# Ten of the 22 gate and value pairs of an up projection computed in seven block products

## The chip, the cores and the metric

One Trainium2 chip, one of its cores. The metric is device time in microseconds, from the start to the end of one execution; shorter is better. The engines are named as in the profile: PE is TensorE (matmuls), PEld its weight loads, DVE VectorE, ACT ScalarE, POOL GpSimd, SP SyncE, which only issues DMAs here.

## What is computed

One layer of an encoder: 512 tokens, 1024 columns, float32. Three sub-layers follow each other, each with a norm before and after and a residual x: token mixing (attention and a gated scan side by side), cross-attention into 256 memory tokens, and a gated MLP with a convolution over positions. The change is in the last one:

```
def conv_ffn(h, w_up, conv_w, conv_b, w_down):
    u = h @ w_up                                    # 512x1024 @ 1024x5632
    up = jnp.pad(u, ((0, 0), (1, 1), (0, 0)))
    acc = conv_b
    for j in range(3):
        acc = acc + up[:, j:j + n] * conv_w[j]
    gate, val = jnp.split(acc, 2, axis=-1)          # 2816 columns each
    return (jax.nn.silu(gate) * val) @ w_down
```

## The kernel before

**Three matmuls for one product.** Every float32 operand is split into a high part (a cast on ScalarE, L111) and a low part (what is left, on VectorE, L112); `mm3` (L185) then does high x high, high x low and low x high.

**Weights come in units.** The host packs nearly all weights into units of 128 x 1024 floats (512 KB). `unit` (L179) takes the next one and lets `issue_ahead` (L175) split units up to three ahead. `issue` (L154) loads a unit on SyncE's queue into a raw tile (`rawp`, two buffers, L140 to L151) and splits it into wh and wl (`wp`, four buffers). 110 units hold the weights up to the up projection, and 42 the products of the down projection. Units 50 to 57 are the queries of cross-attention, 58 to 65 its output projection, 66 to 109 the up projection.

**The up projection.** A tile of the result has 128 columns as partitions and the 512 tokens along its row. There are 22 pairs of a gate tile and a value tile; a tile is 8 blocks of the model dimension x 3 matmuls of 512 columns into one PSUM bank. The first two pairs are computed in two halves of 256 tokens, since the last two blocks of h are transposed (`turn_in`, L224) between their first halves. Then a plain loop over i = 2 to 21 does gate and value of a pair. `conv` (L983) takes each bank: bias and middle tap on ScalarE (L986), the other taps on VectorE (L987, L989), then silu on the gate (L992) or the product with the gate (L1000).

**The down projection** is already computed in seven block products (Strassen-Winograd): `PRODUCTS` names the weight block or sum of blocks of each. The sums of its weight blocks, t1 to t4, are made in DRAM by `new_sums` (L935) after pairs 2, 5, 8 and so on: the first block is copied by ScalarE's queue (t1, t3) or the sum before is copied by GpSimd's (t2, t4), and the second block is added by an accumulating DMA of GpSimd. `group_sides` (L948) makes the sums of the activations for eight pairs at a time.

**What sets the order.** The framework turns the text into one instruction list per engine and adds all waits; among ready instructions the one that is earlier in the text goes first, so instructions of one engine can change places. `tc.issue_after` pins an instruction behind another one on its engine. Of the 8 KB tiles `big` there are 16; of PSUM banks eight, two for each of the tags b, s, c, o. The residual x lies in two `big` tiles from the mixing on to the end.

## Time and profile before

| | |
|---|---|
| median of 3 runs | 828.1 us (827.95 to 830.31) |
| the profiled execution | 828.14 us, of which span 826.4 us |
| instructions | 11158 |
| DMA | 135.64 MB in 40054 packets, mean 164 GB/s |
| HBM | read 130.72 MB, written 25.17 MB |
| weight loads by SyncE (raw<-in_w) | 109 of 512 KB, median 3.9 us from issue to landing |
| first block copied by ScalarE's queue (sum_t<-in_wd) | 10 of 512 KB, 5.1 us |
| accumulating DMAs of GpSimd (sum_t<-in_wd) | 20 of 512 KB, 8.1 us |
| copies of a sum by GpSimd (sum_t<-sum_t) | 10 of 512 KB, 4.6 us |

How to read it: a row of a group of instructions has its line, engine, operation, out<-in with shapes and the count, then busy us and the mean ns of one, then the engine's idle time before it and who ended that. A row of a window has for each engine the busy us and the count, then the granted clock of TensorE (1.00 is full), the mean busy share of the 16 DMA engines, and GB/s. A row of the timeline has start, duration, engine and line. "DMA to landing" has minimum, median and maximum of the time from issue to the last byte. Matmuls are pipelined, and the records of two that follow each other overlap.

### The profile page before, as it was taken

The page shows a single profiled execution, that of the slowest core. Times are in us where ns is not written, and L with a number is a line of the kernel's source. Part 1 is how long each engine was busy: PE and PEld are TensorE (multiplying, and loading weights), DVE is VectorE, ACT ScalarE, POOL GpSimd, SP SyncE. Part 2 cuts the span into 40 slices and gives each one's busy share as a digit, 9 for nine tenths or more (in the row PEclk, how much of TensorE's full clock was granted, in tenths as well). Part 3 has the DMA queues.
Part 4 walks back from the last instruction along what each step waited for, and adds up shares of the span by engine and source line. Part 5 has one row for each costly group of instructions (what it writes and reads, how often), then busy time and mean ns, then how long its engine had stood idle before and what let it go on. Part 6 is the DMA issues. An engine that isn't in the chain of part 4 may idle for free.

```text
span 826.4 us, 11158 instructions
## 1 busy us (share of the span) xinstructions
PE 812.9 (98%) x4238; PEld 689.2 (83%) x4238; DVE 533.9 (65%) x802; ACT 456.3 (55%) x766; POOL 131.4 (16%) x194
## 2 busy tenths in 40 slices
PE   9999999999999999999999999999999999999996
PEld 7878888889898887888888898888888888888884
DVE  5347486569886875855453866557555655888765
ACT  6576756369788874645543554334333343567651
POOL 0110211044223201300000300111111121011302
PEclk9999999999999999999999999999999999999999
DMA  8696754667768533252213136797888996268852
GB/s 317 184 276 136 166 116 98 129 141 158 161 153 182 124 126 130 77 178 77 77 52 102 44 110 179 214 246 201 229 211 228 257 257 167 90 203 270 246 148 102
DMA packets 40054, 135.64 MB, mean 164 GB/s; under 512 B 5120, under 2 KB 7168, under 8 KB 39808
## 3 DMA queue, kind: packets, MB, share of 16 engines
q1 hardware_dynamic: 25632, 86.03, 30.5%
q0 software_dynamic: 11344, 40.38, 26.2%
q10 hardware_dynamic: 3024, 8.53, 3.0%
q8 instruction: 33, 0.54, 0.3%
q14 instruction: 21, 0.17, 0.1%
HBM read 130.72 MB, written 25.17 MB: 189 GB/s over the span
## 4 chain that ended last, share of the span: by engine, by line
PE 91%; DVE 3%; issue 2%; DMA 1%; ACT 1%; POOL 1%; POOLq 0%; DVEq 0%; ACTq 0%
PE ps_b L187 9%; PE ps_b L188 9%; PE ps_b L186 9%; PE ps_s L187 6%; PE ps_s L188 6%; PE ps_s L186 6%; PE ps_o L186 5%; PE ps_o L187 5%; PE ps_o L188 5%; PE ps_c L187 5%; PE ps_c L186 5%; PE ps_c L188 5%; PE ps_c L553 3%; PE ps_o L798 2%; PE ps_s L776 2%
## 5 line engine op out<-in xcount | busy, mean ns | idle before, releaser
L112 DVE TENSOR_TENSOR wl<-raw,wh 128x1024 fp32r<-128x1024 f32 (+1 forms) x93 | 112.2, 1208 | 117.5 <-ACT wh L111 117.3
L111 ACT CAST wh<-raw 128x1024 fp32r<-128x1024 f32 (+1 forms) x93 | 96.0, 1033 | 138.4 <-PE ps_b L187 44.0
L186 PE MATMUL ps_b<-big,wh 128*128 128x512 f32 (+1 forms) x320 | 118.2, 369 | 0.8 <-DVE big L112 0.8
L188 PE MATMUL ps_b<-big,wl 128*128 128x512 f32 (+1 forms) x320 | 116.6, 365 | 0.0
L187 PE MATMUL ps_b<-big,wh 128*128 128x512 f32 (+1 forms) x320 | 116.4, 364 | 0.0
L186 PEld LDWEIGHTS ps_b<-big,wh 128*128 128x128 f32 x320 | 60.4, 189 | 9.7 <-DVE big L112 0.9
L188 PEld LDWEIGHTS ps_b<-big,wl 128*128 128x128 f32 x320 | 60.3, 188 | 9.3
L187 PEld LDWEIGHTS ps_b<-big,wh 128*128 128x128 f32 x320 | 60.4, 189 | 9.1
L579 DVE TENSOR_TENSOR big<-big 128x512 f32<-128x512 f32 x64 | 48.4, 761 | 16.3 <-PE ps_c L553 9.4
L186 PE MATMUL ps_s<-wh,big 128*128 128x512 f32 (+1 forms) x140 | 53.7, 384 | 0.4 <-DVE big L112 0.4
L187 PE MATMUL ps_s<-wl,big 128*128 128x512 f32 (+1 forms) x140 | 53.2, 380 | 0.9 <-DMA wl<-in_w_dram 0.9
L188 PE MATMUL ps_s<-wh,big 128*128 128x512 f32 (+1 forms) x140 | 53.1, 379 | 0.0
L163 ACT CAST wh<-raw 128x1024 fp32r<-128x1024 f32 x35 | 36.8, 1050 | 25.9 <-PE ps_b L187 13.1
L168 POOL DMA_DIRECT2D wl<-in_w_dram x35 | 30.7, 877 | 121.3 <-ACT wl L165 106.3
L112 DVE TENSOR_TENSOR big<-ps_o,big 128x512 fp32r<-128x512 f32 x54 | 37.1, 688 | 13.4 <-ACT big L111 13.2
L111 ACT CAST big<-ps_o 128x512 fp32r<-128x512 f32 x54 | 31.7, 586 | 19.5 <-PE ps_o L901 7.5
L945 POOL DMA_DIRECT2D sum_t<-in_wd_dram x24 | 19.6, 831 | 125.1 <-DMA sum_t<-in_wd_dram 76.1
L186 PE MATMUL ps_o<-wh,big 128*128 128x512 f32 (+1 forms) x102 | 39.4, 386 | 0.0
L992 ACT ACTIVATE tmp<-tmp 128x512 f32<-128x512 f32 x22 | 13.9, 632 | 44.7 <-DVE tmp L989 44.7
L187 PE MATMUL ps_o<-wl,big 128*128 128x512 f32 (+1 forms) x102 | 38.2, 375 | 0.0
L188 PE MATMUL ps_o<-wh,big 128*128 128x512 f32 (+1 forms) x102 | 38.2, 374 | 0.0
L186 PE MATMUL ps_b<-wh,big 128*128 128x512 f32 x92 | 36.9, 402 | 0.0
(267 smaller groups left out, 2062.6 us busy)
## 6 DMA issues: line engine op xcount, KB each, us to landing
raw<-in_w_dram SPq DMA_DIRECT2D x109, 512.0 KB, 3.9
wl<-in_w_dram POOLq DMA_DIRECT2D x35, 512.0 KB, 5.6
sum_t<-in_wd_dram POOLq DMA_DIRECT2D x20, 512.0 KB, 8.1
sum_t<-in_wd_dram ACTq DMA_DIRECT2D x10, 512.0 KB, 5.1
sum_t<-sum_t POOLq DMA_DIRECT2D x10, 512.0 KB, 4.6
big<-sum_t SPq DMA_DIRECT2D x10, 512.0 KB, 4.4
raw<-sum_t SPq DMA_DIRECT2D x10, 512.0 KB, 4.5
big<-in_x_dram SPq DMA_DIRECT2D x8, 512.0 KB, 6.4
```

The costliest lines, as they stand in the source:

```text
L111: nc.scalar.copy(hi, src)
L112: (eng or nc.vector).tensor_sub(lo, src, hi.bitcast(F32))
L163: nc.scalar.copy(wh, raw)
L168: nc.gpsimd.dma_start(wl, io["w"][i], accum_op=ALU.add)
L186: nc.tensor.matmul(o, a[0], b[0], start=start, stop=False)
L187: nc.tensor.matmul(o, a[0], b[1], start=False, stop=False)
L188: last_mm[0] = nc.tensor.matmul(o, a[1], b[0], start=False, stop=stop).ins
L553: nc.tensor.matmul(o[:, b, :], kc[:, blk(b)], pat(qk, b * P, [[2 * m, P // (2 * m)], [T + m, 2], [1, m]]), start=True, stop=True)
L579: nc.vector.tensor_tensor(out=c, in0=c, in1=pat(tt, toff + off, [[2, npair], [gap, 2], [0, m]]), op=ALU.mult)
L776: nc.tensor.matmul(s, qT[h // 4][:, h % 4, blk(qb)], kT[:, 2 * (h // 4) + c, :], start=c == 0, stop=c == 1)
L798: nc.tensor.matmul(o, vv[:, c, h // 4].rearrange("p a d -> p (a d)"), pt[:, j, c, :], start=c + j == 0, stop=c == 3 and j == 1)
L945: nc.gpsimd.dma_start(t, weight_block(second_name, width(u)), accum_op=ALU.add)
```

## The change

Ten pairs (`UP_S`) are computed in seven products as well. The tokens are halved (near, far) and so is the model dimension; gate and value are the two column halves. w11 and w12 are the gate and value blocks of the first half of the model dimension, w21 and w22 those of the second; t1 = w11 + w12, t3 = w22 + w12, t2 = w22 + t1, t4 = w21 + t2. On the side of h there are four sums s1 to s4, made once on VectorE from `fulls`, an unsplit copy of the transposed h that ScalarE now keeps in `turn_in`, and split. Each product is 4 x 3 matmuls of 256 columns. Three banks hold a pair: g (w11, later w21 on top of it, and t4), m (t1, t2), n (w22, t3). VectorE and ScalarE put the products together, and `conv` runs as before, the gate from the bank, the value from a tile.

What the change moves besides:

- The units of these pairs hold two blocks of 256 KB each (the fourth one block). Loads run up to five units ahead, with the two `tmp4` tiles as two more raw buffers.
- The sums of weight blocks, of both projections, become a list of jobs: seeds (a copy of the first block, on SyncE's queue, pinned behind the last weight load) and adds (GpSimd, accumulating), for two pairs or two units of the down projection at a time, eight seeds and then eight adds. Five jobs go with each of units 53 to 60, three with each from unit 70 on. Rows of the sums in DRAM are 32 floats longer than their data.
- x is copied to DRAM by ScalarE's queue after the first two pairs and read back at product 4 of the down projection.
- The first left side of the down projection is made at i = 20, not at i = 8; banks go round by `next_bank`; the host packs the blocks of the ten pairs as `wu`.

```diff
@@ -26,12 +26,18 @@
...
-N_WHOLE, N_UNITS = 110, 152
+UP_S = (4, 6, 7, 9, 11, 12, 14, 16, 17, 19)
+N_MIX, N_WHOLE = 66, 110 - 2 * len(UP_S)
+N_DOWN = N_WHOLE + 4 * len(UP_S)
+N_UNITS = N_DOWN + 42
...
-SUMS = (("t1", "w11", "w12"), ("t3", "w22", "w12"), ("t2", "t1", "w22"), ("t4", "t2", "w21"))
-LAY_AHEAD = 3
+SUMS = (("t1", "w11", "w12"), ("t3", "w22", "w12"), ("t2", "w22", "t1"), ("t4", "w21", "t2"))
+BLOCKS = ("w11", "w12", "w21", "w22")
+UP_PRODUCTS = ("w11", "t2", "t1", "w22", "t3", "w21", "t4")
+JOBS_AHEAD, JOBS_UP, FIRST_JOB, LAST_JOB = 5, 3, 53, 60
+LAY_AHEAD, LOAD_AHEAD = 3, 5
@@ -116,45 +122,76 @@
...
+    def up_block(name, q):
+        if name in BLOCKS:
+            return io["wu"][q, BLOCKS.index(name)]
+        return sums[name, q]
...
+    plan = [[("w", i)] for i in range(N_MIX)]
+    whole = N_MIX
+    for i in range(NF):
+        if i in UP_S:
+            q = UP_S.index(i)
+            for k in range(0, 7, 2):
+                plan.append([("u", q, name) for name in UP_PRODUCTS[k:k + 2]])
+        else:
+            plan += [[("w", whole)], [("w", whole + 1)]]
+            whole += 2
...
+        k = (i - N_DOWN) % 4
+        if k >= 2 and N_MIX + 6 <= i < N_DOWN:
+            return tmp4([P, 1024])
...
     def load_w():
-        i = issued[0]
+        i = loaded[0]
...
-        issued[0] += 1
+            last_load[0] = nc.sync.dma_start(raw, weight_block(PRODUCTS[p][0], cols)).ins
+        elif plan[i][0][0] == "w":
+            last_load[0] = nc.sync.dma_start(raw, io["w"][plan[i][0][1]]).ins
+        else:
+            for k, (_, q, name) in enumerate(plan[i]):
+                while (name, q) not in sums and name not in BLOCKS:
+                    jobs.popleft()()
+                last_load[0] = nc.sync.dma_start(raw[:, half(k)], up_block(name, q)).ins
+            raw = raw[:, :512 * len(plan[i])]
+        loaded[0] += 1
         return raw
...
     def issue():
         i = issued[0]
-        raw = load_w()
+        issued[0] += 1
+        raw = raws.popleft() if raws else load_w()
@@ -169,12 +206,58 @@
...
+        n = JOBS_AHEAD if FIRST_JOB <= i <= LAST_JOB else JOBS_UP if i >= N_MIX + 4 else 0
+        for _ in range(min(n, len(jobs))):
+            jobs.popleft()()
+
+    def sum_jobs(name, n, block):
+        made = {}
+
+        def seed(out_name, first_name):
+            def go():
+                t = dram.tile([P, n + 32], F32, name="sum_%s_%s" % (out_name, name), tag="sum_%s_%s" % (out_name, name))
+                made[out_name] = t[:, :n]
+                with tc.issue_after(last_load[0]):
+                    nc.sync.dma_start(made[out_name], block(first_name))
+            return go
+
+        def add(out_name, second_name, keep):
+            def go():
+                src = made[second_name] if second_name in made else block(second_name)
+                nc.gpsimd.dma_start(made[out_name], src, accum_op=ALU.add)
+                keep(out_name, made[out_name])
+            return go
+        return seed, add
+
+    def plan_sums(rows):
+        made = [sum_jobs(name, n, block) + (keep,) for name, n, block, keep in rows]
+        for out_name, first_name, _ in SUMS:
+            for seed, _, _ in made:
+                jobs.append(seed(out_name, first_name))
+        for out_name, _, second_name in SUMS:
+            for _, add, keep in made:
+                jobs.append(add(out_name, second_name, keep))
...
+    for q in range(0, len(UP_S), 2):
+        plan_up_sums(range(q, min(q + 2, len(UP_S))))
+    for u in range(0, 6, 2):
+        plan_down_sums((u, u + 1))
...
             issue()
+        while N_MIX + 4 <= taken[0] and loaded[0] < min(N_UNITS, taken[0] + LOAD_AHEAD):
+            raws.append(load_w())
@@ -182,10 +265,15 @@
...
+    def mm3(o, a, b, start, stop, again=False):
+        nc.tensor.matmul(o, a[0], b[0], start=start, stop=False, skip_group_check=again)
+        nc.tensor.matmul(o, a[0], b[1], start=False, stop=False, skip_group_check=again)
+        last_mm[0] = nc.tensor.matmul(o, a[1], b[0], start=False, stop=stop, skip_group_check=again).ins
@@ -221,14 +306,14 @@
...
-    def turn_in(h, act, b, tags, before=None):
+    def turn_in(h, act, b, tags, keep=None):
         for c in range(2):
-            if before:
-                before(c)
             o = bank(tags[c]).rearrange("p (k n) -> p k n", k=4)
             for k in range(4):
                 nc.tensor.transpose(o[:, k, :], h[:, blk(c * 4 + k)], ident)
             hi, lo = act.hi, act.lo
+            if keep:
+                nc.scalar.copy(keep[c][:, :, blk(b)], o)
             if len(hi) == 2:
@@ -928,22 +1013,11 @@
...
     hT = new_act()
-    turns = res_second(ox, range(4), kv["x0"], between(x, g_post, g_pre, hT))
+    fulls = [big([P, 4, T]) for _ in range(2)]
+    turns = res_second(ox, range(4), kv["x0"], between(x, g_post, g_pre, hT, fulls))
...
-
-    def new_sums(u):
-        n = width(u).stop - width(u).start
-        for out_name, first_name, second_name in SUMS:
-            t = dram.tile([P, n], F32, name="sum_%s_%d" % (out_name, u), tag="sum_%s_%d" % (out_name, u))
-            if first_name in sums:
-                nc.gpsimd.dma_start(t, weight_block(first_name, width(u)))
-            else:
-                with tc.issue_after(last_act[0]):
-                    nc.scalar.dma_start(t, weight_block(first_name, width(u)))
-            nc.gpsimd.dma_start(t, weight_block(second_name, width(u)), accum_op=ALU.add)
-            sums.setdefault(out_name, []).append(t)
...
-            if i == 8:
+            if i == 20:
                 lay_ahead(1)
@@ -1016,11 +1090,74 @@
...
+    saved = [dram.tile([P, 2, D], F32, name="saved%d" % b, tag="saved%d" % b) for b in range(2)]
+    for b in range(0, NB, 2):
+        rows2 = bass.AP(tensor=x[b].tensor, offset=x[b].offset, ap=[list(x[b].ap[0]), [1, 2 * D]])
+        with tc.issue_after(last_act[0]):
+            nc.scalar.dma_start(saved[b // 2].rearrange("p b n -> p (b n)"), rows2)
+
+    wide = [big([P, 2, 4, 256]) for _ in range(2)]
+    s1, s2, s3, s4 = wide[0][:, 0], wide[0][:, 1], wide[1][:, 0], wide[1][:, 1]
+    (a11, a21), (a12, a22) = [[f[:, :, t] for t in half_t] for f in fulls]
+    sums_of_h = []
+    for o, i0, i1 in ((s1, a21, a22), (s2, a11, s1), (s3, a21, a11), (s4, a12, s2)):
+        nc.vector.tensor_sub(o, i0, i1)
+        t = big([P, 2, 4, 256], F32R)
+        split(t[:, 0], t[:, 1], o)
+        sums_of_h.append((t[:, 0], t[:, 1]))
+    h1, h2 = [(hT.hi[k], hT.lo[k]) for k in range(2)]
+    near, far = half_t
+    left_h = {"w11": (h1, near), "t2": (sums_of_h[1], slice(0, 256)), "t1": (sums_of_h[0], slice(0, 256)),
+              "w22": (sums_of_h[3], slice(0, 256)), "t3": (sums_of_h[2], slice(0, 256)), "w21": (h2, near),
+              "t4": (h2, far)}
+    tag_at = [0]
+
+    def next_bank():
+        tag_at[0] += 1
+        return bank(up_tags[(tag_at[0] - 1) % 4])
+
+    def strassen_pair(i):
+        g, m, n = next_bank(), next_bank(), next_bank()
+        place = {"w11": (g, near), "t2": (m, far), "t1": (m, near), "w22": (n, near), "t3": (n, far),
+                 "w21": (g, near), "t4": (g, far)}
+        two, more, val = tmp2(tag="th"), tmp2(tag="th"), tmp2(tag="tq")
+        for k, name in enumerate(UP_PRODUCTS):
+            if k % 2 == 0:
+                w = take()
+            (hi, lo), cols = left_h[name]
+            o, at = place[name]
+            o = o[:, at]
+            for kc in range(4):
+                wc = slice((k % 2) * 512 + kc * P, (k % 2) * 512 + kc * P + P)
+                mm3(o, (w[0][:, wc], w[1][:, wc]), (hi[:, kc, cols], lo[:, kc, cols]), kc == 0 and name != "w21",
+                    kc == 3, name == "w21")
+            if name == "w11":
+                nc.scalar.copy(two[:, near], o)
+            elif name == "t2":
+                nc.vector.tensor_sub(two[:, far], o, two[:, near])
+            elif name == "t1":
+                nc.vector.tensor_add(more[:, near], o, two[:, far])
+            elif name == "t3":
+                nc.vector.tensor_tensor(out=val.rearrange("p (a t) -> p a t", a=2),
+                                        in0=n.rearrange("p (a t) -> p a t", a=2),
+                                        in1=more[:, None, near].to_broadcast([P, 2, 256]), op=ALU.add)
+                nc.vector.tensor_add(more[:, far], o, two[:, far])
+            elif name == "t4":
+                nc.vector.tensor_sub(o, o, more[:, far])
+        conv(0, i, g)
+        conv(1, i, val)
+
     for i in range(2, NF):
+        if i in UP_S:
+            strassen_pair(i)
+            continue
         for c in range(2):
-            drain(proj_fm(hT, T, up_tags[(2 * i + c) % 4], lambda u: conv(c, i, u)))
-        if i % 3 == 2 and i // 3 < 6:
-            new_sums(i // 3)
+            o = next_bank()
@@ -1078,6 +1210,10 @@
...
         elif p == 4:
+            x = room_x()
+            for b in range(0, NB, 2):
+                rows2 = bass.AP(tensor=x[b].tensor, offset=x[b].offset, ap=[list(x[b].ap[0]), [1, 2 * D]])
+                nc.scalar.dma_start(rows2, saved[b // 2].rearrange("p b n -> p (b n)"))
...
+def pack_up(w_up):
+    w = w_up.reshape(2, 4, P, 2, NF, P).transpose(4, 0, 3, 2, 1, 5)
+    return w.reshape(NF, 4, P, 512)[list(UP_S)]
...
```

63 lines of the change are left out of this document (35 added, 28 removed).

## The prediction

> **What bounds the kernel now.** I read the page's totals and its chain first, then a table of windows over the stages around the up projection, then the matmul timeline at three places in it.
>
> ```profile
> span 826.4 us, 11158 instructions
> PE 812.9 (98%) x4238; PEld 689.2 (83%) x4238; DVE 533.9 (65%) x802; ACT 456.3 (55%) x766; POOL 131.4 (16%) x194
> PE 91%; DVE 3%; issue 2%; DMA 1%; ACT 1%; POOL 1%; POOLq 0%; DVEq 0%; ACTq 0%
> ```
>
> TensorE is busy for 98% of the span and 91% of the chain that ended last is its matmuls. The windows say whether that holds in the stages that the change touches (358 to 455 is cross-attention, 455 to 484 its output projection and the turn into the up projection, 484 to 496 the first two pairs, then the other twenty pairs, then the down products):
>
> ```profile
> core 0: us, PE busy (x) PEld busy (x) DVE busy (x) ACT busy (x) POOL busy (x), PEclk, DMA share, GB/s
> 358.00:455.00 97.00, 97.00 (x487) 81.73 (x487) 45.56 (x67) 42.70 (x90) 3.20 (x8) 1.00 0.28 93
> 455.00:484.14 29.14, 29.14 (x191) 26.43 (x190) 22.32 (x31) 15.45 (x34) 8.38 (x18) 1.00 0.22 73
> 484.14:495.66 11.52, 11.52 (x98) 11.52 (x97) 6.96 (x8) 6.99 (x8) 0.00 (x0) 1.00 0.27 92
> 495.66:713.26 217.60, 217.60 (x962) 180.20 (x961) 130.23 (x152) 84.82 (x104) 27.00 (x38) 1.00 0.77 209
> 713.26:800.00 86.74, 86.74 (x384) 71.82 (x383) 69.11 (x72) 53.92 (x64) 11.66 (x12) 1.00 0.72 216
> 800.00:826.40 26.40, 18.51 (x81) 14.63 (x79) 16.36 (x24) 7.03 (x15) 5.63 (x9) 0.94 0.30 108
> ```
>
> From 358 to 800 us TensorE is busy in all of the time at the full granted clock (1.00). So matmul time taken out of the up projection shortens the kernel one for one, and every wait that the change gives TensorE lengthens it one for one. What else is near its limit in the twenty pairs is the DMA engines (0.77) and then VectorE (130.23 of 217.60); ScalarE and GpSimd are far from it.
>
> **The matmuls.** The pace is read from starts, since a matmul's record is longer than the step to the next.
>
> ```profile
> 484.14 0.28 PE L186 MATMUL ps_b<-big,wh 128*128 128x256 f32 x1
> 495.66 0.40 PE L186 MATMUL ps_b<-big,wh 128*128 128x512 f32 x1
> 713.29 0.39 PE L186 MATMUL ps_b<-wh,big 128*128 128x512 f32 x1
> ```
>
> From 484.14 to 495.66 lie the second token halves of the first four tiles: 4 x 24 = 96 matmuls of 256 columns, 11.52 / 96 = 0.120 us each. From 495.66 to 713.29 lie 40 tiles of 24 matmuls of 512 columns: 217.63 / 960 = 0.2267 us each. A pair now is 48 x 0.2267 = 10.88 us. As seven products it is 7 x 4 x 3 = 84 matmuls of 256 columns, 84 x 0.120 = 10.08 us. Ten pairs save 10 x 0.80 = 8.0 us. The weight load of each short matmul is in this pace already (PEld is busy for 11.52 of 11.52 us there), so this term has no second price. It is also the most that the change can win, as no other stage loses work on TensorE.
>
> The Trainium skill (TensorE: Matmul & The Clock Gate, section "Wait — 56ns, not 53.3ns?") gives columns / 2.4 GHz + about 2.5 ns for a matmul. By it a pair would go from 10.36 to 9.17 us and ten would save an estimated 11.9 us; the trace's 0.120 and 0.2267 us lie about 13 ns above columns / 2.4, so the rule is too kind to many short matmuls here and the trace decides.
>
> **VectorE and ScalarE.**
>
> ```profile
> L112 DVE TENSOR_TENSOR wl<-raw,wh 128x1024 fp32r<-128x1024 f32 x42 | 51.4, 1223 | 72.0 <-ACT wh L111 72.0
> L987 DVE SCALAR_TENSOR_TENSOR tmp<-ps_s,cw,tmp 128x511 f32<-128x511 f32 x11 | 8.2, 747 | 8.3 <-ACT tmp L986 8.3
> L989 DVE SCALAR_TENSOR_TENSOR tmp<-ps_s,cw,tmp 128x511 f32<-128x511 f32 x11 | 8.2, 750 | 0.4
> L1000 DVE TENSOR_TENSOR big<-tmp,tmp 128x512 f32<-128x512 f32 x21 | 14.5, 692 | 0.8
> L112 DVE TENSOR_TENSOR wl<-big,wh 128x512 fp32r<-128x512 f32 x3 | 2.0, 683 | 0.3 <-ACT wh L111 0.3
> L112 DVE TENSOR_TENSOR big<-ps_b,big 128x256 fp32r<-128x256 f32 x8 | 3.4, 420 | 0.1
> L112 DVE TENSOR_TENSOR big<-ps_o,big 128x512 fp32r<-128x512 f32 x54 | 37.1, 688 | 13.4 <-ACT big L111 13.2
> L953 DVE TENSOR_TENSOR big<-big 128x1024 f32<-128x1024 f32 x2 | 2.5, 1226 | 0.1
> L111 ACT CAST wh<-raw 128x1024 fp32r<-128x1024 f32 x42 | 44.1, 1051 | 81.7 <-PE ps_b L187 29.4 <-PE ps_c L187 24.4 <-DMA raw<-in_w_dram 12.2
> ```
>
> A whole pair costs VectorE two weight splits, two convolutions and a product: 2 x 1.22 + 2 x (0.75 + 0.75) + 0.69 = 6.1 us. A pair in seven products has three and a half units to split (3 x 1.22 + 0.68), four sums of 256 columns (4 x 0.42), one of 512 (0.69), and the same convolutions and product (3.7): 10.4 us, against 10.08 us of matmuls. The four sums of h and their four low parts come once, 8 x 1.22 = 9.8 us. Over the twenty pairs that is 130.2 + 10 x 4.3 + 9.8 = 183 of 209.6 us, so it fits. Where it is tight is pairs 2 to 7: 3 x 6.1 + 9.8 + 3 x 10.4 + 3.7 (the first side sums, three as on L953) = 63 us, against 3 x 10.88 + 3 x 10.08 = 62.9 us of matmuls. Lateness there is first taken up by eight PSUM banks (a pair takes three) and four split weight tiles. I put 0.5 us on it, between 0 and 3 (about one convolution that is late). ScalarE gets 1.5 casts and a copy more per pair, some 2 us, and has 84.8 of 217.6 us now: nothing.
>
> Before the first pairs ScalarE also copies eight transposed 128x512 banks. The last two casts of that turn stand here:
>
> ```profile
> 480.85 0.59 ACT L111 CAST big<-ps_c 128x512 fp32r<-128x512 f32 x1 [3.10 <-PE ps_c L230]
> 481.33 0.59 ACT L111 CAST big<-ps_o 128x512 fp32r<-128x512 f32 x1
> ...
> 482.07 0.68 DVE L112 TENSOR_TENSOR big<-ps_o,big 128x512 fp32r<-128x512 f32 x1
> ```
>
> Two copies of 0.59 us ahead of or between them bring the last low part from 482.75 to 483.9. The second token halves start at 484.14 and need that part after 12 matmuls, at 485.6: nothing, and at most 1.2 us if the cover goes.
>
> **The bank that two products share.** This is a new wait. Product t2 goes to the far half of bank m, VectorE subtracts from there, and the next product, t1, writes the near half of the same bank. If it has to stand behind the subtraction, TensorE waits from the pace's end to the record's end (0.28 - 0.12 = 0.16) and for the 0.42 us of the subtraction: 0.6 us, ten times 6 us. Against that speaks that instructions are not issued in the text's order:
>
> ```profile
> 506.77 0.78 ACT L986 ACTIVATE tmp<-ps_s,cw 128x512 f32<-128x512 f32 x1 [1.18 <-PE ps_s L188]
> 507.45 1.04 ACT L111 CAST wh<-raw 128x1024 fp32r<-128x1024 f32 x1
> 511.98 1.05 ACT L111 CAST wh<-raw 128x1024 fp32r<-128x1024 f32 x1 [3.49 <-PE ps_c L187]
> ```
>
> The text has one weight cast ahead of each tile's L986; here two follow each other, since a ready instruction went first. So matmuls of w22 (another bank, weights in the same unit) can be put into the gap. Bounds 0 and 6; I take 2.0, nearer to the lower for that row.
>
> **DMA.** Ten pairs load 70 blocks of 256 KB instead of 20 units of 512 KB, 18.35 MB for 10.49. The sums of their blocks are new, 40 seeds on SyncE's queue and 40 accumulating adds on GpSimd's, 10.5 MB each. The down sums' seeds leave ScalarE's and GpSimd's queues for SyncE's. Forty of the 128 jobs go with units 53 to 60, in cross-attention, where the engines are 0.28 busy: 24 seeds and 16 adds (6.3 and 4.2 MB) are hidden. The rest come three to a unit from unit 70 and are out by unit 99, in pair 11.
>
> ```profile
> q0 software_dynamic: 4000, 17.83, 40.0%
> q1 hardware_dynamic: 6048, 21.76, 28.7%
> q10 hardware_dynamic: 1728, 5.77, 8.0%
> ...
> DMA to landing us min/median/max: 3.1/3.2/4.2
> ...
> DMA to landing us min/median/max: 3.3/5.3/8.2
> ```
>
> The queue rows are of the window of the twenty pairs: SyncE's queue (q1) takes 0.287 x 217.6 / 21.76 = 2.87 us of all 16 engines per MB, GpSimd's (q0), nearly all sums, 0.400 x 217.6 / 17.83 = 4.88. Over the whole stage: 0.77 x 217.6 = 167 now, + 7.9 MB of loads (23), + 4.2 MB of seeds (12), + 4.2 to 6.3 MB of adds (20 to 31), + 2.1 MB of parked residual (6), - 5.8 MB that change from 4.88 to 2.87 (12): about 222 us in 209.6 plus what runs in the 20 us before. It is full. The two landing rows are those of weight loads at L146 from 340 to 405 us, with no sums beside them, and from 505 to 690 us, with sums: up to 8.2 us instead of 3.2. A load here is sent up to eight units ahead of its use with four raw and four split tiles, 10 us or more even at the 2.88 us of a seven-product unit, so 8.2 us is still covered. Bounds 0 and 20 (the rival below); I take 1.5.
>
> Parking the residual: two issues on ScalarE's queue out, two back at product 4, with 15 us of product 5 (66 x 0.2267) before x is needed: nothing. GpSimd's adds stand in its queue with the small norms of the turn; those are ahead in the text. SyncE's loads stand behind seeds that wait for nothing.
>
> **Sum.** -8.0 + 0.5 + 2.0 + 1.5 = -4.0 us. The profiled execution took 828.14 us (span 826.4, 1.7 around it), the median of the runs is 828.1: both give 824.1; I say 824.
>
> **Rivals.** *The sums' transfers hold up the weights (slower).* Up to pair 11, from the first jobs at about 476 us, there are 124 us of matmuls. In them must pass 14.4 MB of loads, 15.7 of seeds and 2.1 of residual (32.2 x 2.87 = 92 us) and 15.7 MB of adds (77 us): 169 us. Less the last eight adds, which nothing near waits for (15), and some 14 that buffers cover: 140 in 124, 16 to 20 us late, 828 - 8 + 18 + 2 = 840 us. For: the landing rows, and loads stand behind seeds in one queue. Against: adds may run late at no cost, SyncE's queue alone needs 92 of 124, and packet times hold some waiting. It decides as soon as the adds take more than about half of the engines while seven-product pairs run. Chance 0.18.
>
> *The shared bank with VectorE's queue in front of it (slower).* If t1 isn't moved, and the subtraction finds a weight split or a convolution of the last pair running (1.22 or 0.75 us, VectorE being full in such a pair), each wait is 0.6 + about 1.2 = 1.8 us, ten 18: 828 - 8 + 18 = 838 us. It decides from 0.8 us per pair. Chance 0.12. The Trainium skill (PSUM — Partial Sum Buffer, section "PSUM bank collisions raise a hardware error") says that two engines may not touch one bank in the same partitions at once, even at other columns, and must be kept apart by a semaphore; by that rule the wait is there. No row of this trace shows the case.
>
> *The gain is eaten (no change).* The 6 us of the bare shared bank, or a few late loads, against 8.0: 826 to 830. Chance 0.18.
>
> *All covered.* 8.0 us won, 820.1. It is the good end of the forecast, which with its bounds (820 to 825.6) has 0.52.
>
> **Range and chances.** Measurements of this kernel can tell about 0.3%, 2.5 us, from no change. Faster by more 0.52 (forecast), within 0.18, slower 0.30 (0.18 + 0.12). The range goes from 819.5 (all covered, and the spread of the runs) to 838, which leaves out the worse half of the slow cases and little below; the forecast's own range is 820 to 825.6.
>
> **What would show it.** Starts of short matmuls 0.120 us apart inside a product; a pair from its w11 to the next pair's first matmul 10.1 to 10.5 us; TensorE still busy for all of 496 to 705. A gap between t2 and t1 names the bank, its length VectorE's share. Idle TensorE before w11, t1 or t3 after a late cast with a DMA as releaser, in pairs 7 to 11 first, and landings of 10 us or more, name the transfers. The forecast is wrong if either sums to over 5 us.

## The result: 6.8% slower

The changed kernel takes 883.4 us in the median of four runs (882.8 to 890.3), the kernel before 828.0 us: a ratio of 1.068, with a 95% interval of 1.063 to 1.074. The profiled execution took 882.82 us.

The page of the changed kernel begins like this:

```profile
span 881.0 us, 12319 instructions
...
PE 823.3 (93%) x4598; PEld 712.7 (81%) x4598; DVE 578.0 (66%) x880; ACT 483.4 (55%) x808; POOL 163.5 (19%) x222
...
PE   9999999999999999999999997784859999999896
...
PEclk9999999999999999999999999786969999999999
DMA  8695644568576232999423799999994454279752
...
PE 62%; DMA 21%; DVE 5%; issue 5%; ACT 3%; POOL 3%; SPq 1%; POOLq 0%; DVEq 0%; ACTq 0%
```

TensorE was busy in 98% of the span and is in 93% now; the transfers, which had 1% of the chain that ended last, have 21%. The row of TensorE dips in slices 25 to 30 (528 to 661 us), where the DMA row stands at 9, and a little near its end (slices 38 and 40). The windows give the sizes (columns as in the prediction: engines, granted clock, DMA share, GB/s):

```profile
358.00:455.00 97.00, 94.55 (x473) 78.78 (x472) 43.57 (x64) 40.76 (x87) 22.39 (x30) 1.00 0.81 221
...
484.00:496.00 12.00, 12.00 (x101) 12.00 (x102) 5.79 (x8) 6.11 (x9) 0.92 (x1) 1.00 0.54 159
496.00:560.00 64.00, 58.53 (x338) 52.67 (x338) 47.49 (x59) 29.14 (x37) 15.51 (x19) 0.95 1.05 300
560.00:620.00 60.00, 39.99 (x210) 35.64 (x209) 27.36 (x37) 16.13 (x21) 9.75 (x12) 0.74 1.05 301
620.00:680.00 60.00, 47.20 (x275) 42.51 (x274) 35.21 (x48) 22.45 (x29) 7.67 (x10) 0.86 0.84 240
680.00:740.00 60.00, 60.00 (x409) 55.84 (x408) 48.53 (x67) 30.53 (x40) 0.00 (x0) 1.00 0.47 151
```

From 496 to 620 the DMA engines are full (1.05: the share adds up the times of packets, and these overlap a little), and TensorE is idle for 25.5 us of 124 and runs at a clock of 0.95 and 0.74. From 680 on, with the sums out, TensorE is busy in all of the time at the full clock, with VectorE at 48.53 of 60: the seven-product pairs themselves run as they should.

Three points of the matmul timeline divide the loss: the last transposes of the turn, the first down product, the end.

| | last transposes | from there to the first down product | from there to the end |
|---|---|---|---|
| before | 481.0 us | 232.3 us | 113.1 us |
| after | 484.8 us | 280.4 us | 115.9 us |
| difference | +3.8 | +48.0 | +2.8 |

The middle stage should have taken 232.3 - 8.0 = 224.3 us; it is 56 us over that. Of the 56, 38.3 us are idle TensorE between 496 and 680 (5.47 + 20.01 + 12.80 from the windows); the other 17.8, by subtraction, are matmuls at the lower clock that follows the waits (the steps from matmul to matmul in the trace come to 18.0 us over the full pace).

What the transfers did from 496 to 650 us (queues: packets, MB, share of 16 engines; issues: count, KB each, median us to landing):

```profile
q0 software_dynamic: 5512, 15.29, 51.9%
q1 hardware_dynamic: 11779, 28.26, 50.1%
q10 hardware_dynamic: 288, 2.10, 3.3%
...
raw<-sum_t_u SPq DMA_DIRECT2D x11, 256.0 KB, 13.0
...
raw<-in_wu_dram SPq DMA_DIRECT2D x7, 256.0 KB, 13.2
...
tmp<-in_w_dram SPq DMA_DIRECT2D x2, 512.0 KB, 16.9
```

105.3% of 154 us is 162 us of all 16 engines. The matmuls that this work stands beside are those of pairs 2 to 11, five whole and five in seven products: 5 x 10.88 + 5 x 10.08 = 104.8 us. 162 - 105 = 57 us, and the stage is 56 us late: these pairs, which lie between 499.3 and 659.7 us in the matmul timeline, take as long as the transfers beside them. That alone would be weak evidence, since packet times in a stretch with full engines add up to about its length whatever the cause; but at the prices read before the change (2.87 and 4.88 us per MB) the same bytes come to 161 us too (81 for SyncE's queue, 75 for GpSimd's, 5 for q10). GpSimd's queue, nearly all accumulating adds, took 80 us of it at 5.23 us per MB; SyncE's took 77 us at 2.73. Weight loads land after 10 to 17 us (medians of their groups); in the same window of the kernel before it was 5.1.

The loads are also sent late. SyncE's own waits in this kernel (line waited for: us in total, times, longest us; L179 and L184 issue weight loads, L221 seeds):

```profile
SPq L184 <- DMA sum_t_d<-in_wd_dram: 17.9, 10, 3.5
SPq L221 <- DMA sum_t_d<-in_wd_dram: 15.2, 8, 3.5
SPq L179 <- DMA sum_t_d<-in_wd_dram: 9.2, 3, 3.4
```

What lands here are seeds of the down sums, and 27 us of these waits stand in front of a weight load. From 496 to 650 SyncE issued 81 transfers, 59 of them with seven earlier ones of its own still in flight, never with more; then it waited until one had landed, 87 us in all, nearly none of it for an add of GpSimd. So a load waits twice: in line behind seeds, and then for its own packets among those of the adds.

How a late load reaches TensorE, in three views of the longest wait. ScalarE, VectorE and TensorE, each with the idle time before an instruction and its releaser:

```profile
645.76 1.56 ACT L117 CAST wh<-raw 128x1024 fp32r<-128x1024 f32 x2 [5.51 <-DMA raw<-in_wu_dram]
```

```profile
646.83 1.83 DVE L118 TENSOR_TENSOR wl<-raw,wh 128x1024 fp32r<-128x1024 f32 x2 [5.87 <-ACT wh L117]
648.58 0.74 DVE L1061 SCALAR_TENSOR_TENSOR tmp<-ps_s,cw,tmp 128x511 f32<-128x511 f32 x1
649.36 0.75 DVE L1063 SCALAR_TENSOR_TENSOR tmp<-ps_s,cw,tmp 128x511 f32<-128x511 f32 x1
650.02 0.42 DVE L1137 TENSOR_TENSOR tmp<-ps_o,tmp 128x256 f32<-128x256 f32 x1
```

```profile
650.49 0.58 PE L274 MATMUL ps_o<-big,wh 128*128 128x256 f32 x1 [8.25 <-DVE tmp L1137]
```

The weight load is 5.5 us late; the cast, the split, two convolutions of the pair before and the subtraction of t2 (L1137) stand in line behind it; and t1 waits for that subtraction because of the bank that they share. TensorE's wait names VectorE, but the first cause is a DMA. Whether the shared bank made the wait longer or only gave it its name, the trace can't say: that is one of the questions below.

### The profile page after: what moved, and what is told of

Read it like the earlier page. It is cut to its first block, busy times and chain, and to the rows that moved or that the text cites. A ratio compares the mean times of both kernels' runs of the same rounds, so it can differ in the third digit from the quotient of the medians.

```text
span 881.0 us, 12319 instructions
## 1 busy us (share of the span) xinstructions
PE 823.3 (93%) x4598; PEld 712.7 (81%) x4598; DVE 578.0 (66%) x880; ACT 483.4 (55%) x808; POOL 163.5 (19%) x222
## 4 chain that ended last, share of the span: by engine, by line
PE 62%; DMA 21%; DVE 5%; issue 5%; ACT 3%; POOL 3%; SPq 1%; POOLq 0%; DVEq 0%; ACTq 0%
PE ps_b L274 6%; PE ps_b L275 6%; PE ps_b L276 6%; DMA raw<-sum_t_u 5%; PE ps_s L275 4%; PE ps_s L276 4%; PE ps_s L274 4%; DMA raw<-in_w_dram 4%; PE ps_o L274 4%; PE ps_o L275 4%; PE ps_o L276 4%; DMA sum_t_d<-in_wd_dram 3%; DMA raw<-in_wu_dram 3%; PE ps_c L638 3%; PE ps_c L274 3%
## 5 line engine op out<-in xcount | busy, mean ns | idle before, releaser
L118 DVE TENSOR_TENSOR wl<-raw,wh 128x1024 fp32r<-128x1024 f32 (+1 forms) x83 | 95.9, 1158 | 99.9 <-ACT wh L117 99.5
L117 ACT CAST wh<-raw 128x1024 fp32r<-128x1024 f32 (+1 forms) x83 | 82.7, 998 | 127.2 <-DMA raw<-in_w_dram 32.1
L274 PE MATMUL ps_b<-big,wh 128*128 128x512 f32 (+1 forms) x352 | 126.2, 358 | 9.1 <-ACT wh L117 3.6
L275 PE MATMUL ps_b<-big,wh 128*128 128x512 f32 (+1 forms) x352 | 123.5, 351 | 0.0
L274 PEld LDWEIGHTS ps_b<-big,wh 128*128 128x128 f32 x352 | 68.2, 194 | 18.6 <-ACT wh L117 3.8
L275 PEld LDWEIGHTS ps_b<-big,wh 128*128 128x128 f32 x352 | 68.1, 193 | 7.7
L117 ACT CAST wh<-tmp 128x1024 fp32r<-128x1024 f32 (+1 forms) x30 | 29.7, 990 | 54.1 <-DMA tmp<-in_wu_dram 11.7
L274 PE MATMUL ps_o<-big,wh 128*128 128x256 f32 (+1 forms) x120 | 40.4, 337 | 16.3 <-DVE tmp L1137 8.2
L118 DVE TENSOR_TENSOR wl<-tmp,wh 128x1024 fp32r<-128x1024 f32 (+1 forms) x30 | 34.5, 1149 | 27.6 <-ACT wh L117 27.4
L274 PE MATMUL ps_c<-big,wh 128*128 128x256 f32 (+1 forms) x124 | 40.7, 328 | 12.2 <-DVE tmp L1137 8.1
L274 PE MATMUL ps_s<-big,wh 128*128 128x256 f32 (+1 forms) x132 | 43.4, 329 | 1.3 <-DVE tmp L1137 1.3
L275 PE MATMUL ps_s<-big,wh 128*128 128x256 f32 (+1 forms) x132 | 43.1, 327 | 0.0
L276 PE MATMUL ps_s<-big,wl 128*128 128x256 f32 (+1 forms) x132 | 43.1, 326 | 0.0
```

The costliest lines, as they stand in the source:

```text
L117: nc.scalar.copy(hi, src)
L118: (eng or nc.vector).tensor_sub(lo, src, hi.bitcast(F32))
L274: nc.tensor.matmul(o, a[0], b[0], start=start, stop=False, skip_group_check=again)
L275: nc.tensor.matmul(o, a[0], b[1], start=False, stop=False, skip_group_check=again)
L276: last_mm[0] = nc.tensor.matmul(o, a[1], b[0], start=False, stop=stop, skip_group_check=again).ins
```

## The experiments

The theories, as the expectations name them. **A**: the DMA engines are full, and loads wait for seeds and adds. **B**: the bank that t1 and t2 share. **C**: VectorE is full in such a pair. **D**: loads stand behind seeds in SyncE's one queue. **E**, formed after the first runs: a late load's split, in VectorE's fixed order, holds the subtraction of t2, so that the shared bank passes on a lateness which the buffers would have covered.

Where no interval is given, the time is of one execution, beside the kernel before at 827.3 to 827.8 us. The columns are those of the profiled execution.

| run | us | last transposes | to the first down product | to the end |
|---|---|---|---|---|
| no_up_sums | 834.2 | 481.4 | 233.5 | 117.6 |
| no_adds | 825.6 | 482.2 | 225.5 | 116.1 |
| few_seeds | 877.7 | 504.8 | 255.8 | 115.3 |
| two_jobs | 867.4 | 487.3 | 261.1 | 117.2 |
| own_bank | 880.6 | 485.6 | 277.1 | 116.1 |
| paced | 862.4 | 486.5 | 254.9 | 119.3 |
| paced_own | 852.9 | 486.0 | 243.9 | 121.3 |
| no_park | 823.1 | 480.9 | 225.9 | 114.5 |
| pool_sums | 825.2 | 482.0 | 228.3 | 113.1 |
| pool9 (profiled) | 833.5 | 482.2 | 233.1 | 116.4 |
| pool9g (profiled) | 835.3 | 483.2 | 234.8 | 115.5 |
| late_keep (profiled) | 825.0 | 480.2 | 229.4 | 113.6 |

The column of the last transposes holds scatter from stages that no run changes. The first transposes of the same kind in a kernel, long before the MLP, start at 129.8 us in the kernel before and anywhere from 128.0 to 130.9 in these runs. The turn itself, from its first transposes to its last, takes 21.6 us before, 22.4 in late_keep, 25.1 in pool9g, and 22.7 in every other version.

**Without the sums of up weights** (no_up_sums).

```diff
-JOBS_AHEAD, JOBS_UP, FIRST_JOB, LAST_JOB = 5, 3, 53, 60
+JOBS_AHEAD, JOBS_UP, FIRST_JOB, LAST_JOB = 0, 1, 53, 60
...
-        if name in BLOCKS:
-            return io["wu"][q, BLOCKS.index(name)]
-        return sums[name, q]
+        return io["wu"][q, {"t1": 1, "t2": 3, "t3": 1, "t4": 2}.get(name, 0) if name not in BLOCKS else BLOCKS.index(name)]
...
-    for q in range(0, len(UP_S), 2):
-        plan_up_sums(range(q, min(q + 2, len(UP_S))))
```

> The ten pairs load plain blocks in place of the sums t1 to t4, so no sum is made for the up projection; the down sums go one job to a unit from unit 70. This leaves out part of the weights' arithmetic. Theory A (the DMA engines are full from 498 to 650 us and loads wait for seeds and adds): nothing is late any more, ten pairs at 10.1 to 10.2 us, 820 to 825 us. Theory B (the bank that t2 and t1 share) and theory C (VectorE full in such a pair): the waits of 0.6 to 1.8 us per pair stay, 826 to 838 us.

Measured: 834.2 us. Of the 56 us in the middle stage 47 went (280.4 to 233.5), but A's 820 to 825 was too low. Windows, the matmul timeline and a row of the issues from 496 to 650 of this run:

```profile
496.00:560.00 64.00, 62.83 (x395) 56.90 (x394) 53.88 (x70) 32.27 (x41) 6.09 (x8) 1.00 0.90 283
560.00:620.00 60.00, 55.66 (x359) 51.34 (x358) 45.05 (x60) 27.39 (x35) 7.68 (x10) 0.97 0.92 278
```

```profile
579.44 0.39 PE L268 MATMUL ps_c<-big,wh 128*128 128x256 f32 x1 [4.34 <-DVE tmp L1131]
```

```profile
raw<-in_w_dram SPq DMA_DIRECT2D x6, 512.0 KB, 12.5
```

The number fits B and C as well (826 to 838). But late loads remain, with the sums of the down weights and a mean DMA share of 0.9: 12.5 us for units of 512 KB, about 8 for blocks of 256 KB. A mean share of 0.9 over 60 us is not a tenth of room for each load. The next run decides.

**Without the accumulating adds** (no_adds): all loads, all seeds and all arithmetic of the seven products stay.

```diff
-                nc.gpsimd.dma_start(made[out_name], src, accum_op=ALU.add)
```

> All 64 accumulating adds are left out, the seeds stay where they are (the sums are then only their first blocks). Theory A: 162 us of engine time between 496 and 650 us less about 80 us of adds leaves 82 in the 106 us that the pairs 2 to 11 need; little or nothing late, 822 to 830 us. Theory D (the loads are late because they stand behind seeds in SyncE's one queue, whatever GpSimd does): most of the 56 us stay, 860 to 880 us. B and C: 883 us.

Measured: 825.6 us.

```profile
496.00:560.00 64.00, 64.00 (x405) 58.23 (x404) 54.20 (x69) 33.79 (x43) 1.17 (x2) 1.00 0.91 314
560.00:620.00 60.00, 59.78 (x382) 54.42 (x382) 51.46 (x70) 31.10 (x40) 0.00 (x0) 1.00 0.73 250
```

Taking out one line takes out 58 us. The middle stage is 225.5 us, 1.2 over the 224.3 of matmul pace: that is all that the shared bank (B) and VectorE (C) cost when loads are in time, and both are out as the cause. D as it was put, whatever GpSimd does, is out too, since the seeds still stand in SyncE's queue ahead of the loads, and SyncE waited only 12 us for transfers of its own. What this run does not take apart is the pair of them: seeds that land slowly because of the adds hold the loads in line. It also shows what the change was worth without its adds: 825.6 against 827.8, and 823.1 with x left in its place (below).

**Small seeds, whole adds** (few_seeds): the first block is copied in 16 columns only, into 16 tiles of DRAM that are used again and again, the loads read plain blocks, and six jobs go with each of units 53 to 60 in place of five.

```diff
-                    nc.sync.dma_start(made[out_name], block(first_name))
+                    if full:
+                        nc.sync.dma_start(made[out_name], block(first_name))
+                    else:
+                        nc.sync.dma_start(made[out_name][:, :16], block(first_name)[:, :16])
```

> Nearly all seeds are cut to 16 columns, the adds stay whole and go into 16 tiles of DRAM again and again; the loads read plain blocks. This leaves out part of the weights' arithmetic. Theory A: 162 less about 37 us of seeds is 125 us of engine time in 106: some 20 us late, 840 to 850 us. Theory D: the loads have their queue to themselves, 820 to 830 us. B and C: 883 us.

Measured: 877.7 us, neither. The middle stage is 255.8 us, 25 us less than with whole seeds, and still 31 us over; I had given A 20. What I had not seen is that adds which no longer wait for seeds crowd into cross-attention:

```profile
358.00:455.00 97.00, 79.84 (x399) 67.24 (x398) 38.58 (x60) 37.52 (x80) 20.97 (x26) 0.91 0.83 206
...
560.00:620.00 60.00, 45.51 (x290) 42.62 (x290) 36.81 (x49) 20.83 (x28) 14.37 (x18) 0.89 1.06 233
```

TensorE loses 17 us there in a window whose mean DMA share is only 0.83, and the last transposes are 24 us later than before. Nor does the run decide on D (820 to 830). A small seed has to wait until the adds into the same tile are done: SyncE stood still for 31 us in such waits between 496 and 650, the longest 12.3, with loads behind it. But loads that were sent landed late here too (8.3 and 8.4 us for blocks, medians), with next to no seed bytes in their queue, so adds do slow loads directly. No run moves the seeds, whole, to another queue; how the 56 us divide between the full engines and the line behind the seeds stays open.

**Two jobs per unit in place of three** (two_jobs).

```diff
-JOBS_AHEAD, JOBS_UP, FIRST_JOB, LAST_JOB = 5, 3, 53, 60
+JOBS_AHEAD, JOBS_UP, FIRST_JOB, LAST_JOB = 5, 2, 53, 60
```

> Two jobs instead of three with each unit from unit 70 on, so the last goes with unit 113 in pair 14 instead of unit 99 in pair 11. Theory A: about 175 us of engine time from 498 on must pass before pair 15, which without waits begins at 638 us: about 35 us late in place of 56, 860 to 868 us, and the full stretch ends later. B and C: 883 us, as no pair changes.

Measured: 867.4 us, as A has it. The same transfers, spread over more matmuls, cost 16 us less.

**t2 in a bank of its own** (own_bank).

```diff
-        g, m, n = next_bank(), next_bank(), next_bank()
-        place = {"w11": (g, near), "t2": (m, far), "t1": (m, near), "w22": (n, near), "t3": (n, far),
+        g, d, m, n = next_bank(), next_bank(), next_bank(), next_bank()
+        place = {"w11": (g, near), "t2": (d, near), "t1": (m, near), "w22": (n, near), "t3": (n, far),
```

> The changed kernel with product t2 in a bank of its own, so that t1 no longer has to follow VectorE's subtraction of t2. Everything else as it is. Theory A (the DMA engines are full, the loads come late, and nothing else matters): the loads come no sooner, 878 to 886 us, with the same length of gaps under other names. Theory E (loads are late, and on top of that the split of a late load, up to three units ahead, holds the subtraction behind it in VectorE's fixed order, so that the shared bank passes on a lateness that the buffers would have covered): no gap names the subtraction any more, and 10 to 25 us go: 858 to 873 us. Theory B (the bank alone) is out by the run without adds; it would give 830.

Measured: 880.6 us, 2.7 us below the median of the changed kernel and 2.2 below its fastest run. No wait of TensorE names the subtraction any more, and the time changes next to nothing. The matmul timeline of this run, where the changed kernel waited 8.25 us until 650.49:

```profile
650.48 0.58 PE L274 MATMUL ps_s<-big,wh 128*128 128x256 f32 x1 [4.38 <-ACT wh L117]
```

It is another product of the same pair, t3 in place of t1, so the nearly equal start is chance: this run is some 18 short matmuls further. But its wait names the weights. E's 10 to 25 us do not come in the changed kernel: nearly all that is not lost at the bank is lost at the next weights.

**Jobs spread wider** (paced), **and that with the bank of its own** (paced_own).

```diff
-        n = JOBS_AHEAD if FIRST_JOB <= i <= LAST_JOB else JOBS_UP if i >= N_MIX + 4 else 0
+        n = JOBS_AHEAD if FIRST_JOB <= i <= LAST_JOB else (3 if i >= N_DOWN or plan[i][0][0] == "w" else 1) if i >= N_MIX + 4 else 0
```

> The changed kernel with the same jobs spread wider: from unit 70 on three with a unit of whole columns but one with a unit of blocks, so that they are out near pair 18, not 11. Theory A: the stage from the turn to the first down product then needs about the transfers of the whole stage (222 us of all engines, worked out ahead) in 224 us of matmuls, so most of the lateness goes: 832 to 848 us, with the DMA share even at 0.9 to 1.0 over all 20 pairs in place of 1.05 and then 0.47. Theory E with A: the same sign, and gaps at the subtraction stay where a single load is late. Theory D (the loads stand behind the seeds in one queue): seeds are still ahead of loads, two thirds of the lateness stays, over 860 us.

> Both: jobs spread wider, and t2 in a bank of its own. Theory A alone: as the spread version, within 2 us. Theory E: 3 to 12 us less than the spread version, 826 to 840 us, with the stage from the turn to the first down product at 226 to 235 us.

Measured: 862.4 and 852.9 us. Both are above A's range (832 to 848, 826 to 840). The windows of the first say why:

```profile
560.00:620.00 60.00, 50.00 (x307) 45.81 (x306) 39.12 (x51) 22.73 (x29) 7.85 (x10) 0.89 0.97 278
620.00:680.00 60.00, 49.44 (x308) 45.19 (x308) 38.33 (x53) 23.17 (x31) 8.96 (x11) 0.91 1.00 287
680.00:740.00 60.00, 57.64 (x344) 51.94 (x344) 47.51 (x63) 30.13 (x38) 5.27 (x7) 0.97 0.66 201
```

A job of the down sums is 512 KB, twice one of the up sums. Two seeds and two adds of that size cost 2.1 MB, half at 2.73 and half at 5.23 us per MB, 8.3 us of all engines, and the loads of a seven-product pair another 1.83 x 2.73 = 5.0: 13 us beside 10.1 us of matmuls. I had spread the jobs by number, not by bytes, and the engines stay nearly full from 496 to 680 (0.95 in the first of these windows). Here the second bank is worth 9.5 us, 11 in the middle stage, and the four waits that name the subtraction in paced, 22.9 us together, are gone in paced_own. That speaks for E as a second-order effect; it is one run of each, and four runs of the changed kernel lie up to 7.5 us apart. The down stage pays too (119.3 and 121.3 us in place of 115.9); that some of the sums are then still being made is the likely reason, which no run takes apart.

**x not parked** (no_park): the version without adds once more, and x stays in its tiles.

```diff
-            nc.scalar.dma_start(saved[b // 2].rearrange("p b n -> p (b n)"), rows2)
...
-                nc.scalar.dma_start(rows2, saved[b // 2].rearrange("p b n -> p (b n)"))
```

> The version without the accumulating adds once more (it leaves the second blocks out of all sums, and took 825.6 us), and x stays in its two tiles instead of going to DRAM and back. Theory P (the down stage is 3 us longer because the tiles that x leaves and takes again change which transfer a left-side cast waits for): the stage from the first down product to the end goes from 116.1 to about 113.1 us as in the kernel before, 822.0 to 823.2 us in all. Rival (the longer down stage comes from the order in which the sums are made, or from the left side that is made at pair 20): 116 us there, 825 to 826 us.

Measured: 823.1 us, 2.4 us less than without adds, at theory P's upper end, but by luck: the down stage gives only 1.5 us of it (116.1 to 114.5, not 113.1). The last transposes come 1.3 us sooner because all of the kernel runs ahead by as much from 130 us on, which is scatter. 1.5 us of the longer down stage stay open.

**Sums on the chip** (pool_sums): seven pairs; their four blocks are loaded, and GpSimd adds them in SBUF. The products come in another order, x is not parked, and all seeds of the down sums go out in cross-attention.

```diff
-UP_S = (4, 6, 7, 9, 11, 12, 14, 16, 17, 19)
+UP_S = (3, 5, 7, 9, 11, 13, 15)
...
+        for o, i0, i1 in ((t1, w11, w12), (t3, w22, w12), (t2, w22, t1), (t4, w21, t2)):
+            last_sum[0] = nc.gpsimd.tensor_tensor(out=o, in0=i0, in1=i1, op=ALU.add).ins
```

> A version without the sums of up weights in DRAM: seven pairs (3, 5, 7, 9, 11, 13, 15) in seven products, whose four blocks are loaded as whole units of 1 MB a pair, as in the kernel before, and whose four sums GpSimd makes on the chip, 4 x 128x512; the sums of the down weights stay in DRAM, 24 seeds with units 53 to 60, the adds four to a pair; x is not parked. Matmuls save 7 x 0.80 = 5.6 us. If the traffic of the sums is what cost the time (A, E): the loads land as before, 822 to 826 us. If GpSimd needs over 2.5 us for a sum, or VectorE is slowed beside it, or the late sums reach the shared bank (E by another way): 828 to 845 us, with gaps at the subtraction and GpSimd's sums as releaser.

Measured: 825.2 us. Two windows, GpSimd's groups over the whole run and the issues from 496 to 650:

```profile
496.00:560.00 64.00, 63.13 (x395) 57.04 (x395) 55.42 (x66) 32.62 (x41) 26.48 (x23) 1.00 0.72 172
560.00:620.00 60.00, 60.00 (x372) 54.16 (x371) 51.59 (x64) 28.45 (x38) 27.62 (x24) 1.00 0.78 190
```

```profile
L187 POOL TENSOR_TENSOR tmp<-raw,tmp 128x512 f32<-128x512 f32 x14 | 21.4, 1531 | 0.5
L187 POOL TENSOR_TENSOR tmp<-raw 128x512 f32<-128x512 f32 x14 | 20.4, 1468 | 92.6 <-DVE tmp L1134 38.8 <-DMA raw<-in_wu_dram 26.2 <-PE ps_c L273 15.7
```

```profile
raw<-in_w_dram SPq DMA_DIRECT2D x18, 512.0 KB, 3.8
raw<-in_wu_dram SPq DMA_DIRECT2D x24, 256.0 KB, 3.3
```

The same product scheme without the DRAM sums has no late load (3.3 and 3.8 us), and TensorE is busy throughout 560 to 620. GpSimd's adds for the down sums still take 42.3% of the engines from 496 to 650, but SyncE has no seeds there. That fits A from the other side, and the line behind the seeds as well. The gain that is left is small: the middle stage is 228.3 us against 226.7 by pace (232.3 - 5.6), and the turn takes 1.1 us more.

**Nine pairs** (pool9), **and GpSimd in place of ScalarE for the copy of h** (pool9g).

```diff
-UP_S = (3, 5, 7, 9, 11, 13, 15)
+UP_S = (4, 6, 8, 10, 12, 14, 16, 18, 20)
```

```diff
-                nc.scalar.copy(keep[c][:, :, blk(b)], o)
+                nc.gpsimd.tensor_tensor(out=keep[c][:, :, blk(b)], in0=hi[c][:, :, blk(b)].bitcast(F32),
+                                        in1=lo[c][:, :, blk(b)].bitcast(F32), op=ALU.add)
```

> The version whose sums GpSimd makes on the chip, with nine pairs (4, 6 and so on to 20) in place of seven from pair 3 on. Matmuls save 9 x 0.80 = 7.2 us; the 1.4 us of idle TensorE that the version with seven had at its first such pair (for the sums of h) should go with the later start, the 1.1 us in the turn stays. Theory A (transfers were the cost, now gone): 822.0 to 823.5 us. If GpSimd's six us per pair or VectorE in every second pair run late: 824 to 828 us.

> The same, and the copy of the transposed h is not made by ScalarE between its casts in the turn but by GpSimd afterwards, as high plus low part, eight sums of 128x512 (about 1.5 us each). If the 1.1 us in the turn is the ScalarE copies that the last low part waits for: 0.8 to 1.2 us less than the version before, 821.0 to 822.5 us. If GpSimd's sums come in the way of its small norms there: the last turn is later, 823 to 826 us.

Measured: 832.6 us (ratio to before 1.0054, 1.0041 to 1.0068) and 836.3 us (1.011, 1.009 to 1.013). Both expectations fell. Two windows of pool9:

```profile
496.00:560.00 64.00, 63.19 (x362) 55.71 (x361) 58.68 (x65) 31.55 (x41) 27.39 (x24) 1.00 0.63 154
...
680.00:740.00 60.00, 57.88 (x303) 49.38 (x302) 51.68 (x63) 33.07 (x41) 7.24 (x6) 1.00 0.50 164
```

With the DMA share at 0.63, VectorE is busy for 58.68 of 64 us, and TensorE's waits of 0.1 to 1.3 us up to 720 us, 6.6 us in all, name VectorE's splits and a convolution; the middle stage is 8.0 us over its pace (225.1). Here C is the likely bound, though no run takes the side sums, which fall into the same pairs, away from it. GpSimd's copies made the turn 2.4 us longer (25.1 in place of 22.7).

**ScalarE's copy of h after its cast, not before** (late_keep, on pool_sums).

> The version with seven pairs and the sums on GpSimd (825.2 us in one run), but ScalarE keeps its copy of the transposed h after the cast and not before it, so that VectorE can take the low part, and give the bank back, 0.6 us sooner. If the 1.2 us of idle TensorE before the last transposes is the copy that stands ahead of the cast: 0.4 to 0.7 us less in the turn, 824.4 to 825.0 us, against 827.4 for the kernel before: faster by 0.3 to 0.4%. Rival (the bank is held until the copy has read it too, in either order): no change, 825.2 us.

Measured: 826.8 us in the median of 12 runs against 827.0 us, ratio 0.9996 (0.9985 to 1.0007): no change. The last transposes come 1.9 us sooner than in pool_sums (480.2 and 482.0), but 1.75 of that is there already at 130 us; the turn itself is 0.35 us shorter, short of the 0.4 to 0.7 expected, and the middle stage is longer by 1.2 us. The single 825.2 us of pool_sums is within the spread of these 12 runs (824.8 to 828.9), so no version here is shown to beat the kernel before.

## Why the prediction was wrong, point by point

**TensorE bounds the kernel, ten pairs save 8.0 us.** Right. Without adds the middle stage is 6.8 us shorter than before, and from 680 us on the changed kernel runs without a wait.

**VectorE in pairs 2 to 7 (0.5 us) and the shared bank (2.0 us).** Right in size: forecast 2.5, and 1.2 us together in the run without adds, where the one wait that names the subtraction is 0.2 us. The rival that made the bank cost 18 us is out by the same run.

**DMA (1.5 us).** This is the step that failed: it cost some 55 us, the 48 of the middle stage and the 8 that were won, less 1 for bank and VectorE. The prices were good: 2.87 and 4.88 us per MB were forecast, 2.73 and 5.23 measured. The first rival had the mechanism and nearly the sum, 169 us of transfers; it counted 15.7 MB of adds where 24 blocks and the down sums, by the same count of jobs, leave 17.8 MB, 10 us more at its price. It had a chance of 0.18. That the sums' transfers cost this is shown by the run without adds; how much came through the full engines and how much through SyncE's line behind the seeds stays open. Three steps took the weight from the rival:

- "adds may run late at no cost". They may, but their packets still hold the engines. From 496 to 650 they took 80 us of 154 while loads landed after 13 us, and without them the kernel takes 825.6. The Trainium skill (DMA: Bandwidth & Descriptors, section "🔬 Queues, rings and completion order") says that an engine goes round between the queues that have work, packet by packet; the two queues' near-equal shares here (51.9% and 50.1%) fit a turn-taking without priority, though adds also wait for seeds, so no run isolates the rule.
- "Less the last eight adds, which nothing near waits for (15), and some 14 that buffers cover", in 124 us. Nothing of the 29 us came off, and of the 20 us ahead of pair 2, from 476 to 496, 8 stayed unused (DMA share 0.59). The working that holds is 162 us of transfers against the 105 us of matmuls of the pairs that stand beside them.
- A load is sent "up to eight units ahead of its use" and "8.2 us is still covered". The kernel lets a load run five units ahead (`LOAD_AHEAD`), 14 us at 2.88 us each, which would cover one load of 8.2. But work came in faster than it went out: a block sent at 496.4 us landed after 4.6, one sent at 575.6 after 22.8. Buffers only delay the first wait. And "SyncE's loads stand behind seeds that wait for nothing" fails: seeds and loads alike waited there for earlier transfers to land.

**Forty jobs hidden in cross-attention.** Wrong by 2.5 us: TensorE is idle for that long from 358 to 455 us (94.55 of 97), and the last transposes are at 484.8 us, without adds at 482.2. A load waits here as well (ScalarE's timeline):

```profile
392.13 1.05 ACT L117 CAST wh<-raw 128x1024 fp32r<-128x1024 f32 x1 [7.42 <-DMA raw<-in_w_dram]
393.09 0.59 ACT L953 ACTIVATE big<-ps_b 128x512 fp32r<-128x512 f32 x1
```

The cast waits 7.4 us for its load, and the evictions of queries behind it wait too. A share of 0.28 before left room for 70 us of transfers in 97, but not for a burst: in the DMA row of the page the slices from 352 to 418 us (17 to 19) stand at 9.

**Copies of h in the turn at nothing, 1.2 us at most.** It is nearly the most: the turn takes 1.1 us more in every version with ScalarE's copy ahead of the cast (22.7 in place of 21.6), 0.9 of it idle TensorE ahead of the last transposes. **Parking x at nothing.** 1.5 us by no_park, in the down stage. The likely reason is not the reload itself but that, with x out of its tiles, they change hands in another order. In the changed kernel ScalarE's cast for a left side waits 6.5 us for a tile that an accumulating DMA still holds, and weight casts stand behind it:

```profile
813.65 1.05 ACT L117 CAST big<-big 128x1024 fp32r<-128x1024 f32 x1 [6.45 <-DMA big<-big]
814.60 1.05 ACT L1043 CAST big<-big 128x1024 fp32r<-128x1024 f32 x1
815.55 1.04 ACT L117 CAST wh<-raw 128x1024 fp32r<-128x1024 f32 x1
```

**The signs named in the prediction** were the right ones to look at: landings over 10 us, idle TensorE after late casts. They begin at 546 us, in pair 6, one pair before those that it named.

## What to carry to other kernels

When transfers are moved or added, compare engine time with matmul time over the very stretch in which both must happen, not over the stage, and take nothing off for transfers that nobody waits for: they share the engines, and here also a queue, with those that somebody waits for. An accumulating sum in DRAM costs its seed and then, for the add, about twice the engine time of a plain transfer of the same bytes (5.23 against 2.73 us per MB here); where an idle engine can add on the chip, the loads stay as they were. A wait that names a bank or an engine may only be the last link: give that resource away in one run before believing it.

## What the runs showed of the hardware

After a wait of some microseconds the matmuls themselves are slower. From the matmul timeline of the changed kernel, a wait of 5.5 us and what follows:

```profile
551.64 0.58 PE L274 MATMUL ps_c<-big,wh 128*128 128x256 f32 x1 [5.47 <-DVE tmp L1137]
552.02 0.41 PE L275 MATMUL ps_c<-big,wh 128*128 128x256 f32 x1
552.23 0.41 PE L276 MATMUL ps_c<-big,wl 128*128 128x256 f32 x1
...
557.57 0.29 PE L274 MATMUL ps_s<-big,wh 128*128 128x256 f32 x1
557.69 0.29 PE L275 MATMUL ps_s<-big,wh 128*128 128x256 f32 x1
```

```profile
552.00:557.50 5.50, 5.50 (x27) 5.50 (x27) 2.37 (x3) 1.04 (x1) 0.81 (x1) 0.50 1.07 271
```

For 5.6 us the step is 0.213 us in place of 0.120, at a granted clock of 0.50: the wait of 5.5 us costs some 2.4 us more, 26 x (0.213 - 0.120). The waits of 0.1 to 1.3 us in pool9 have no such stretch (clock 1.00). The Trainium skill (TensorE: Matmul & The Clock Gate, section 🔬 Part 1: The HAM clock gate) gives half the clock after an idle window of about 3.4 us and the full one after as long a busy window; the half clock agrees, the slow stretch here is longer than that one window. In sums of waits a long one is thus dearer than it looks: 38.3 us of idle time came with about 17.8 us of slow matmuls.

GpSimd adds 128x512 floats in 1.5 us, and 23 such sums beside VectorE's work left the loads at 3.3 to 3.8 us and TensorE busy in 123.1 of 124 us from 496 to 620.
